# Layer 0's modulation on TensorE: weight blocks as the stationary operand instead of the conditions

## The chip, the cores and the metric

The kernel runs on one core of a Trainium2 chip, as one launch. The metric is device time in microseconds (us), the median of several runs of the whole program. Engines are TensorE (PE; its weight loads are listed apart as PEld), VectorE (DVE), ScalarE (ACT), GpSimd (POOL) and SyncE (SP), whose queue issues most of the loads from HBM. Everything is fp32; "fp32r" is the same 32 bits in a form that TensorE multiplies in one pass instead of two.

## The reference, cut to what matters

A block of two layers over 2048 latent tokens and 256 context tokens, 1024 wide. Layer 0 is an attention layer whose input is normalised and then modulated; the shift and scale come from two condition vectors, `c` for the latent and `c_ctx` for the context tokens:

```python
def modulate(x, g, shift, scale):
    return rms_norm(x, g) * (1 + scale) + shift

def ada_params(cond, w, b):                 # w: 1024 x 3072
    m = jax.nn.silu(cond) @ w + b
    return jnp.split(m, 3, axis=-1)         # shift, scale, gate

# layer 0
mods_x = ada_params(c, ada_w[0], ada_b[0])
mods_c = ada_params(c_ctx, ada_w[0], ada_b[0])
hx = modulate(x, norm_g, shift_x, scale_x)
hc = modulate(ctx, norm_g, shift_c, scale_c)
px = hx @ w_in                              # all projections of layer 0
...
```

Nothing of layer 0 can be projected before shift and scale are known. The gates (the last third of `m`) and layer 1's modulation are needed much later and are computed elsewhere.

## The kernel before, in words

`first_mods` (L210 to L232) computes shift and scale of layer 0 for both conditions. It is the first work of the program. `cs` [128, 8, 2] holds the two conditions as columns, eight blocks of 128 input rows, after a SiLU. The weight `ada0` (1024 x 2048, 8 MB) comes in eight blocks k of 128 rows (1 MB each), every block in two halves h of 1024 columns (L219, SP queue). The blocks go round four slots of the buffer `start`, so block 4 waits until TensorE has read block 0. For each half, two matmuls (L221) take `cs[:, k, :]`, 128 rows x 2 columns, as the stationary operand and stream 512 columns of weights past it; four PSUM tiles `ada` (tag "mm", 5 buffers) hold 2 rows x 512 sums each over all eight k. An fp32 matmul runs as two passes, each with its own weight load, so the profile counts 64 for 32 matmuls. Then the four row tiles are copied to `rows` (L224, by turns on VectorE and ScalarE), and 16 small matmuls against a 2x2 identity (L227) turn 2 x 128 pieces into columns: `cols` (tag "tr", 3 buffers) gets 128 partitions x 2 columns for each of 16 column groups. VectorE copies them out as `mods` (L230), and `ada_mods` (L172) adds the bias and forms `shift` and `gs`, per partition, for `load_group`.

`load_group` (L277) brings four token tiles: load `xt`, normalise to `xn` (L206, L208), transpose by TensorE into "tr" tiles (L288), apply `gs` and `shift` from PSUM to `h` (L296 on ScalarE, L293 on VectorE), split `h` into a high and a low half (`ghl`, L48 and L53). `load_w` (L302) brings projection weights `wraw` (2 buffers) and splits them into `whi` on GpSimd (L50) and `wlo` on VectorE (L53). The projections are three fp32r matmuls a step (L57 to L59). `weight_transform` (L234) puts the Fourier layer's weights through a small DFT: it loads `wuT` pieces into the same buffer `start` (L243), adds and subtracts them on VectorE (L246, L247), multiplies on TensorE (L255 to L257), copies on ScalarE (L258, L259).

In this part of the kernel the order of the instructions on each engine and on the DMA queues is set by the framework's planner, which simulates the program's timeline; waits between engines follow from the data. Engines take their instructions strictly in that order. Only the attention phase, from some 800 us on, has an order written out by hand (`P2ORDER`).

Of the kernel before, what the change touches and what calls it, by code (L numbers as in the profile page):

```python
# [10 lines left out]
F32 = mybir.dt.float32  # L11
# [7 lines left out]
P = 128  # L19
D = 1024  # L20
KT = D // P
# [67 lines left out]
def block_kernel(ctx: ExitStack, tc: tile.TileContext, a):  # L89
    nc = tc.nc  # L90
    V, S, T, Q = nc.vector, nc.scalar, nc.tensor, nc.gpsimd
# [33 lines left out]
    ident = const.tile([P, P], F32, name="ident")  # L125
# [46 lines left out]
    def ada_mods(l, m, i):  # L172

        V.tensor_tensor(out=shift[:, i, :], in0=m[:, 0:8], in1=adab[:, l, 0:8], op=ALU.add)
        V.tensor_tensor(out=gs[:, i, :], in0=m[:, 8:16], in1=adab[:, l, 8:16], op=ALU.add)
        V.scalar_tensor_tensor(out=gs[:, i, :], in0=gs[:, i, :], scalar=1.0, in1=ngc[:, l, :],
                               op0=ALU.add, op1=ALU.mult)
# [32 lines left out]
    def first_mods(pool, buf, pp):  # L210

        cs = pool.tile([P, KT, 2], F32, name="cs")
        ld(cs, a["ccT"])
        S.activation(cs, cs, AF.Silu)
        acc = [pp.tile([P, 512], F32, name="ada", tag="mm", bufs=5) for _ in range(4)]
        for k in range(KT):
            aw = buf[:, (k % 4) * 2048:(k % 4 + 1) * 2048]
            for h in range(2):
                ld(aw[:, h * 1024:(h + 1) * 1024], a["ada0"][k * P:(k + 1) * P, h * 1024:(h + 1) * 1024])  # L219
                for q in (2 * h, 2 * h + 1):  # L220
                    T.matmul(acc[q][0:2, :], cs[:, k, :], aw[:, q * 512:(q + 1) * 512], start=k == 0, stop=k == KT - 1)  # L221
        rows = pool.tile([2, 4, 512], F32, name="rows")
        for q in range(4):
            (S.copy if q % 2 else V.tensor_copy)(rows[:, q, :], acc[q][0:2, :])  # L224
        cols = pp.tile([P, 4, P], F32, name="cols", tag="tr", bufs=3).rearrange("p a b -> p (a b)")
        for j in range(16):
            T.matmul(cols[:, 2 * j:2 * j + 2], rows[:, j // 4, (j % 4) * P:(j % 4 + 1) * P], ident[0:2, 0:2],  # L227
                     start=True, stop=True)
        m = pool.tile([P, 2, 16], F32, name="mods")
        V.tensor_copy(m, cols[:, 0:32].rearrange("p (j c) -> p c j", c=2))  # L230
        for c in range(2):
            ada_mods(0, m[:, c, :], c)  # L232
# [30 lines left out]
    with ExitStack() as ph:  # L263
        pp = ph.enter_context(tc.tile_pool(name="p1ps", bufs=4, reuse_waits="tile", space=PSUM))
# [6 lines left out]
        start = grp.tile([P, 2 * KT * G], F32, name="start", tag="ghl")  # L271
        with tc.tile_pool(name="p0", bufs=1, reuse_waits="tile", side="right") as p0:
            first_mods(p0, start, pp)
# [152 lines left out]
        for half in range(2):  # L426
# [4 lines left out]
            for kind, col in chunks:  # L431
                whi, wlo = load_w(col)
                for src, g in groups:
# [4 lines left out]
                    if kind == "g":  # L438
                        if src == 1:
                            continue  # L440
                        for m in range(4):
                            ps = pp.tile([P, 512], F32, name="mm", tag="mm", bufs=5)
                            cs = slice(m * P, (m + 1) * P)
# [59 lines left out]
    with ExitStack() as ph:  # L503
        pp = ph.enter_context(tc.tile_pool(name="p2ps", bufs=1, reuse_waits="tile", space=PSUM))
# [333 lines left out]
    with ExitStack() as ph:  # L838
        pp = ph.enter_context(tc.tile_pool(name="p3ps", bufs=2, reuse_waits="tile", space=PSUM))
# [31 lines left out]
        for g in TOKEN_GROUPS:  # L871
            cs = slice(g * G, (g + 1) * G)
            us = []
            for b in range(KT):
# [13 lines left out]
                h = up.tile([P, G], F32R, name="uh", tag="uh")  # L888
# [188 lines left out]
        with ExitStack() as pd:  # L1077
            pp = pd.enter_context(tc.tile_pool(name="p5ps", bufs=2, reuse_waits="tile", space=PSUM))
# [78 lines left out]
        pp = ph.enter_context(tc.tile_pool(name="p6ps", bufs=2, reuse_waits="tile", space=PSUM))  # L1157
# [180 lines left out]
```

## Time and profile before

| | us |
|---|---|
| runs, median | 2697.39 |
| runs, lowest and highest | 2694.66, 2704.54 |
| profiled execution, time | 2701.17 |
| profiled execution, span from the first to the last instruction | 2699.4 |
| TensorE busy in it | 2593.4 (96%) |
| VectorE, ScalarE, GpSimd busy | 1795.5, 1388.4, 1067.0 |

The time of a run includes a little around the span. Times in the views are us from the span's start. A timeline row gives start, duration, engine, line, operation, written tile and read tiles, shape, and how many instructions are merged in it; in brackets stands the idle time before it and what ended that. Waits and DMA issues are not counted as busy. Ends of matmuls are modelled, so distances between starts are more exact than ends.

### The profile page before, as it was taken

The numbers are of one execution on the slowest core, as the hardware profiler recorded it, in microseconds if no ns is written. First come the engines' busy times: TensorE is split into PE (matmuls) and PEld (weight loads), VectorE is DVE, ScalarE is ACT, GpSimd is POOL, SyncE is SP. The second block draws the span as 40 slices with busy tenths as digits, with TensorE's granted clock in tenths as the row PEclk, the third lists the DMA queues.
The fourth block names the chain that finished last, engine by engine and source line by source line (L and its number), as shares of the span: only waits on it lengthen the run. The fifth ranks groups of instructions, "written<-read, shape, count | busy, mean of one in ns | idle before, by whom it ended". The sixth has DMA issues, their size and how long they took to land.

```text
span 2699.4 us, 44939 instructions
## 1 busy us (share of the span) xinstructions
PE 2593.4 (96%) x15361; PEld 2248.5 (83%) x15361; DVE 1795.5 (67%) x3894; ACT 1388.4 (51%) x3721; POOL 1067.0 (40%) x984
## 2 busy tenths in 40 slices
PE   7899999999998999999999999999999999899998
PEld 3788887787886999999999999999877878688787
DVE  4653734647416888888888888888865444563765
ACT  3621212412216888888888888888824442231212
POOL 1031421233315997666556556566511222332000
PEclk9999999999998999999999999999999999999999
DMA  7547555476534443311151011110287666757542
GB/s 289 192 131 205 149 156 196 118 187 182 146 114 148 160 162 106 112 32 33 35 165 31 29 32 59 54 30 29 86 283 263 207 217 218 254 172 210 195 152 94
DMA packets 294855, 380.20 MB, mean 141 GB/s; under 512 B 26642, under 2 KB 178914, under 8 KB 294626
## 3 DMA queue, kind: packets, MB, share of 16 engines
q1 hardware_dynamic: 163844, 275.02, 31.5%
q10 hardware_dynamic: 125600, 93.38, 11.1%
q0 software_dynamic: 5184, 8.93, 1.2%
q8 instruction: 123, 2.02, 0.3%
q14 instruction: 104, 0.85, 0.1%
HBM read 258.62 MB, written 118.57 MB: 140 GB/s over the span
## 4 chain that ended last, share of the span: by engine, by line
PE 62%; DMA 6%; DVE 4%; issue 1%; ACT 1%; POOL 1%; SPq 0%; DVEq 0%; ACTq 0%; POOLq 0%
PE s L571 17%; PE ptr L671 9%; PE mm L57 7%; PE mm L58 7%; PE mm L59 7%; PE pv L57 5%; PE pv L59 5%; PE pv L58 5%; DMA hraw<-h 1%; DMA wraw<-in_wg 1%; DMA w0h<-wo0h 1%; DVE m L579 1%; DMA wraw<-wur 1%; DMA kB<-kB 1%; DMA rcp<-s1r 1%
## 5 line engine op out<-in xcount | busy, mean ns | idle before, releaser
L579 DVE TENSOR_REDUCE m<-s 128x1 f32<-128x512 f32 (+1 forms) x960 | 579.0, 632 | 170.4 <-PE s L571 162.5
L591 ACT ACTIVATE e<-s,nm 128x512 f32<-128x512 f32 (+1 forms) x960 | 614.1, 653 | 53.1 <-DVE nm L583 50.6
L675 ACT CAST th<-ptr 128x512 fp32r<-128x512 f32 x576 | 340.3, 591 | 135.0 <-PE ptr L671 118.8
L679 DVE TENSOR_TENSOR tl<-ptr,th 128x512 fp32r<-128x512 f32 x576 | 379.1, 681 | 37.3 <-ACT th L675 37.3
L671 PE MATMUL ptr<-ident,e 128*128 128x128 f32 x2304 | 346.7, 273 | 8.8 <-DVE tl L679 6.9
L633 POOL TENSOR_TENSOR e<-e 128x768 f32<-128x768 f32 x189 | 342.6, 1841 | 0.0
L671 PEld LDWEIGHTS ptr<-ident,e 128*128 128x128 f32 x2304 | 270.1, 140 | 37.1 <-DVE tl L679 5.7
L571 PE MATMUL s<-kB,qh 128*128 128x512 f32 (+1 forms) x768 | 285.3, 381 | 10.4 <-DMA kB<-kB 7.3
L50 POOL TENSOR_SCALAR whi<-wraw 128x1024 fp32r<-128x1024 f32 (+1 forms) x104 | 125.4, 1209 | 424.8 <-PE mm L58 123.3
L59 PE MATMUL mm<-whi,ghl 128*128 128x512 f32 x688 | 272.2, 397 | 3.8 <-DVE ghl L53 3.8
L57 PE MATMUL mm<-whi,ghl 128*128 128x512 f32 x688 | 271.9, 398 | 3.8 <-DVE ghl L52 1.9
L58 PE MATMUL mm<-wlo,ghl 128*128 128x512 f32 x688 | 272.1, 397 | 0.7 <-DVE wlo L53 0.7
L630 POOL TENSOR_SCALAR e<-e,rs 128x768 f32<-128x768 f32 x192 | 170.7, 914 | 255.8 <-DVE rs L606 246.7
L53 DVE TENSOR_TENSOR wlo<-wraw,whi 128x1024 fp32r<-128x1024 f32 (+1 forms) x104 | 132.3, 1275 | 183.3 <-POOL whi L50 181.4
L571 PE MATMUL s<-kB,ql 128*128 128x512 f32 (+1 forms) x768 | 252.3, 341 | 0.0
L630 POOL TENSOR_SCALAR e<-e,c 128x768 f32<-128x768 f32 x189 | 168.6, 909 | 139.0 <-ACT e L591 77.0
L333 POOL TENSOR_TENSOR t<-qn,rope 128x256 f32<-128x256 f32 (+1 forms) x128 | 112.3, 898 | 270.3 <-issue 127.5
L591 ACT ACTIVATION_READ_ACCUMULATOR e<-s,nm 128x1 f32 x960 | 201.9, 210 | 0.0
L57 PE MATMUL pv<-th,vAh 128*128 128x256 f32 x576 | 169.0, 293 | 0.2 <-ACT oT L644 0.2
L57 PE MATMUL pv<-th,vBh 128*128 128x256 f32 x576 | 165.5, 287 | 0.0
L571 PEld LDWEIGHTS s<-kB,qh 128*128 128x128 f32 x768 | 147.5, 192 | 19.2 <-DMA kB<-kB 6.1
L58 PE MATMUL pv<-tl,vAh 128*128 128x256 f32 x576 | 160.2, 278 | 0.0
(367 smaller groups left out, 6311.1 us busy)
## 6 DMA issues: line engine op xcount, KB each, us to landing
wraw<-in_w_in SPq DMA_DIRECT2D x56, 512.0 KB, 4.3
hraw<-h SPq DMA_DIRECT2D x96, 256.0 KB, 4.5
aw<-in_adaT SPq DMA_DIRECT2D x64, 256.0 KB, 3.6
g<-sg ACTq DMA_DIRECT2D x64, 256.0 KB, 3.0
gl<-g SPq DMA_DIRECT2D x64, 256.0 KB, 5.3
wraw<-in_wg SPq DMA_DIRECT2D x64, 256.0 KB, 4.2
kB<-kB SPq DMA_DIRECT2D x24, 384.0 KB, 3.8
start<-in_ada SPq DMA_DIRECT2D x16, 512.0 KB, 10.2
```

The lines of the kernel that those rows point to most:

```text
L53: (lo_eng or nc.vector).tensor_tensor(out=lo, in0=src, in1=hi.bitcast(F32), op=ALU.subtract)
L57: nc.tensor.matmul(out, lh, rh, start=start, stop=False)
L58: nc.tensor.matmul(out, lh, rl, start=False, stop=False)
L59: nc.tensor.matmul(out, ll, rh, start=False, stop=stop)
L571: T.matmul(ps[:, c - o:c - o + cw], l, r[c // KP][:, k:k + cw], start=(j == 0), stop=(j == len(self.terms) - 1))
L579: V.tensor_reduce(out=self.m3[:, i:i + 1], in_=self.segs[i][:, 0:SEG[i][1]], axis=AX.X, op=ALU.max)
L591: S.activation(self.e[:, o:o + w], self.segs[i][:, 0:w], AF.Exp, bias=self.nm, accum_out=self.s3[:, i:i + 1])
L630: eng.tensor_scalar(out=self.e[:, sg], in0=self.e[:, sg], scalar1=by, scalar2=1.0, op0=ALU.mult, op1=ALU.mult)
L633: eng.tensor_tensor(out=onto[:, sg], in0=onto[:, sg], in1=self.e[:, sg], op=ALU.add)
L671: T.transpose(self.tr[:, k, i, :], self.p.es[i][:, kt * P:(kt + 1) * P], ident)
L675: S.copy(self.th, self.tr.rearrange("p k i q -> p k (i q)"))
L679: V.tensor_tensor(out=self.tl, in0=self.tr.rearrange("p k i q -> p k (i q)"), in1=self.th.bitcast(F32), op=ALU.subtract)
```

## The change

The weights become the stationary operand: for every block k and each of the 16 groups of 128 weight columns, one matmul holds a 128 x 128 block of `ada0` and streams the two conditions past it as two columns. The sums come out as columns at once, in 32 columns of one PSUM tile `cols`, which is now allocated at the beginning; it collects over all k in one accumulation group, opened by the first matmul and closed by the last. The row tiles, their copies and the 16 matmuls against the identity are gone. Loads of weights, `mods` and what follows stay as they are.

```diff
-        acc = [pp.tile([P, 512], F32, name="ada", tag="mm", bufs=5) for _ in range(4)]
+        cols = pp.tile([P, 4, P], F32, name="cols", tag="tr", bufs=3).rearrange("p a b -> p (a b)")
         for k in range(KT):
             aw = buf[:, (k % 4) * 2048:(k % 4 + 1) * 2048]
             for h in range(2):
                 ld(aw[:, h * 1024:(h + 1) * 1024], a["ada0"][k * P:(k + 1) * P, h * 1024:(h + 1) * 1024])
-                for q in (2 * h, 2 * h + 1):
-                    T.matmul(acc[q][0:2, :], cs[:, k, :], aw[:, q * 512:(q + 1) * 512], start=k == 0, stop=k == KT - 1)
-        rows = pool.tile([2, 4, 512], F32, name="rows")
-        for q in range(4):
-            (S.copy if q % 2 else V.tensor_copy)(rows[:, q, :], acc[q][0:2, :])
-        cols = pp.tile([P, 4, P], F32, name="cols", tag="tr", bufs=3).rearrange("p a b -> p (a b)")
-        for j in range(16):
-            T.matmul(cols[:, 2 * j:2 * j + 2], rows[:, j // 4, (j % 4) * P:(j % 4 + 1) * P], ident[0:2, 0:2],
-                     start=True, stop=True)
+                for j in range(8 * h, 8 * h + 8):
+
+                    T.matmul(cols[:, 2 * j:2 * j + 2], aw[:, j * P:(j + 1) * P], cs[:, k, :],
+                             start=k == 0 and j == 0, stop=k == KT - 1 and j == 15)
         m = pool.tile([P, 2, 16], F32, name="mods")
         V.tensor_copy(m, cols[:, 0:32].rearrange("p (j c) -> p c j", c=2))
```

## Rows read from the trace of the kernel before

**Rows 1.** The page: span, and busy time of each engine.

```profile
span 2699.4 us, 44939 instructions
PE 2593.4 (96%) x15361; PEld 2248.5 (83%) x15361; DVE 1795.5 (67%) x3894; ACT 1388.4 (51%) x3721; POOL 1067.0 (40%) x984
```

**Rows 2.** Timeline, all engines, 0 to 75 us: start, duration, engine, line, operation.

```profile
11.40 15.46 PE L221 MATMUL ada<-start,cs 128*2 128x512 f32 x32 [11.40 <-DMA start<-in_ada]
12.21 0.13 PEld L221 LDWEIGHTS ada<-start,cs 128*2 128x2 f32 x1 [0.73 <-issue]
13.06 0.13 PEld L221 LDWEIGHTS ada<-start,cs 128*2 128x2 f32 x1 [0.73 <-issue]
...
15.11 0.09 PEld L221 LDWEIGHTS ada<-start,cs 128*2 128x2 f32 x1 [0.34 <-issue]
15.54 0.09 PEld L221 LDWEIGHTS ada<-start,cs 128*2 128x2 f32 x1 [0.34 <-issue]
...
28.04 1.88 PE L221 MATMUL ada<-start,cs 128*2 128x512 f32 x4 [1.18 <-DMA start<-in_ada]
30.67 12.18 PE L221 MATMUL ada<-start,cs 128*2 128x512 f32 x28 [0.75 <-DMA start<-in_ada]
```

**Rows 3.** Windows: us, busy by engine (count), granted clock, DMA share, GB/s.

```profile
34.00:37.00 3.00, 3.00 (x8) 0.59 (x7) 0.00 (x0) 0.00 (x0) 0.00 (x0) 1.00 1.03 412
48.30:48.60 0.30, 0.25 (x3) 0.01 (x1) 0.30 (x4) 0.00 (x0) 0.00 (x0) 1.00 1.06 376
48.60:48.90 0.30, 0.00 (x0) 0.00 (x0) 0.30 (x5) 0.00 (x0) 0.00 (x0) 0.70 1.11 382
85.00:90.00 5.00, 3.60 (x31) 3.20 (x29) 2.32 (x7) 5.00 (x26) 0.00 (x0) 1.00 0.30 95
102.00:103.00 1.00, 0.00 (x0) 0.00 (x0) 0.00 (x0) 0.00 (x0) 0.00 (x0) 1.00 0.96 367
107.00:108.00 1.00, 1.00 (x5) 1.00 (x5) 0.97 (x2) 0.00 (x0) 0.00 (x0) 0.50 1.08 374
```

**Rows 4.** Timeline of weight loads and matmuls, 42 to 49; line L227's durations (min/median/max).

```profile
44.77 2.75 PEld L227 LDWEIGHTS cols<-ident,rows 2*128 2x128 f32 x24 [0.17 <-issue]
47.90 0.65 PE L288 MATMUL tr<-ident,xn 128*128 128x128 f32 x4 [0.28 <-DVE mods L230]
L227 PEld LDWEIGHTS cols<-ident,rows x32: 181/187/188, 42.8 to 47.3; 2*128 2x128 f32 x32
```

**Rows 5.** Timeline, 47 to 56: from the columns to the first projection matmul.

```profile
47.65 0.19 DVE L230 COPY mods<-cols 128x32 f32<-128x32 f32 x1 [0.61 <-PE cols L227]
47.82 0.69 DVE L246 TENSOR_TENSOR start<-start 128x512 f32<-128x512 f32 x1
...
48.80 1.22 DVE L53 TENSOR_TENSOR wlo<-wraw,whi 128x1024 fp32r<-128x1024 f32 x1
...
50.61 0.24 DVE L176 SCALAR_TENSOR_TENSOR gs<-gs,ngc 128x8 f32<-128x8 f32 x2
50.80 0.81 ACT L296 ACTIVATE h<-tr,shift,gs 128x128 f32<-128x128 f32 x2 [4.35 <-DVE gs L176]
...
55.27 0.77 PE L57 MATMUL mm<-whi,ghl 128*128 128x512 f32 x1
```

**Rows 6.** Timeline of TensorE's matmuls: the longest idle time up to 110 us.

```profile
106.98 0.80 PE L255 MATMUL wur<-start 128*128 128x129 f32 x2 [6.05 <-DVE start L247]
```

**Rows 7.** Timeline of weight loads at clock 0.50 (to 113.4) and 1.00.

```profile
107.36 0.55 PEld L256 LDWEIGHTS wur<-start 128*128 128x128 f32 x2
107.79 0.55 PEld L257 LDWEIGHTS wur<-start 128*128 128x128 f32 x2
113.69 0.30 PEld L256 LDWEIGHTS wur<-start 128*128 128x128 f32 x2
113.91 0.30 PEld L257 LDWEIGHTS wur<-start 128*128 128x128 f32 x2
```

**Rows 8.** The view of line L221: durations in ns (min/median/max).

```profile
L221 PE MATMUL ada<-start,cs x64: 590/592/1057, 11.4 to 42.3; 128*2 128x512 f32 x64
```

## Prediction

> **What bounds the kernel now.** I began with the page's first lines: TensorE is busy for 2593.4 of 2699.4 us [rows 1]. So what is gained or lost at the start should be found again at the end unless a later idle stretch of TensorE swallows it. The change touches only the first 50 us, so I read the timeline of that stretch next. The 64 passes of L221 (32 matmuls, two passes each in fp32) start at 11.40, when the first weight block lands, and end at about 42.8: the last 28 passes, from 30.67, take 12.18 us, so they start every 0.43 us [rows 2]. On the way TensorE waits for weights twice, up to 28.04 and up to 30.67 [rows 2]; the DMA engines are full meanwhile [rows 3]. Then L227 turns the rows into columns, 32 passes in two stretches with 8 transposes between them, until 47.6, and VectorE copies the result at 47.65 [rows 4, 5]. From there a chain runs to the first projection matmul at 55.27: shift and gs, h, the cast, L57 [rows 5]. After it TensorE is hardly idle until it waits for the second half of the Fourier weights at 106.98 [rows 6]. What sets the time of the change is therefore when the sums over `ada0` are complete, plus that chain.
>
> **Removed.** The 64 passes of L221 with 512 moving columns; four copies of rows, two on VectorE and two on ScalarE, done by the time L227 goes on; and 32 passes of L227. From the first pass to the end of L227 that is 47.6 - 11.4 = 36.2 us, waits for DMA and 8 transposes included.
>
> **Added.** 8 blocks k x 16 column groups = 128 matmuls, 256 passes. Each loads a stationary block of 128x128 and streams two columns. The nearest row in shape is L227 itself, with 128 stationary columns and two moving ones: 24 loads in 2.75 us, the last alone 0.187, so (2.75 - 0.187)/23 = 0.111 us from one pass to the next [rows 4]. It has only 2 partitions where the change has 128. But L256, 128x128 stationary with 64 moving columns, starts its pairs 0.22 us apart from the next line's at full clock, 0.11 us a pass [rows 7]: full partitions cost no more. A pass is thus paid by its weight load, and the two moving columns cost next to nothing. At full clock the stream costs 256 x 0.111 = 28.4 us, less than the 36.2 us now.
>
> **The clock decides.** All turns on whether this stream gets 2.4 GHz or 1.2 GHz. At the lower level the same weight loads cost twice as much: L256 starts at 107.36 and L257 at 107.79, two passes in 0.43 us, 0.215 each, at a granted clock of 0.50 [rows 3, 7]. Then 256 x 0.215 = 55.0 us. The trace has two observations. First, the kernel begins at the lower level: the passes of L221 start 0.85 us apart at 12.21 and 13.06, but 0.43 apart from 15.11 on [rows 2]. (The granted-clock column shows 1.00 for that beginning, so I trust the durations there, where the longest pass is 1057 ns and the median 592 [rows 8].) Dense passes of 512 columns raised it. Second, L227 with its two-column passes ran almost without a gap to 47.6, and four transposes to 48.55; the granted clock fell from 1.00 to 0.50 inside 48.60:48.90, when TensorE had been empty for no more than a few tenths [rows 3, 4]. Two other places show that short idleness alone doesn't do that: in 85:90 it was idle for 1.4 us of 5 and kept 1.00, and in 102:103, without a single matmul, it still had 1.00 [rows 3]. So the row says that back-to-back weight loads with two moving columns do not hold the clock; all the less should they raise it from the low level where the kernel starts. What speaks against: L227 uses 2 partitions, the change 128. No row shows two columns on 128 partitions for that long. I take the low level for the whole stream.
>
> The Trainium skill's page "TensorE: Matmul & The Clock Gate", section "Why this matters for your kernels", advises to keep TensorE continuously busy, without idle gaps between bursts, and the clock stays up. By that rule the new stream, which has no gaps, would run at 2.4 GHz; the fall at 48.7 directly behind a nearly gapless stretch does not agree with it, and the first rival below is worked out for the case that it holds. The same page's section "LDWEIGHTS (loading the stationary operand)" gives a weight load as its columns over 1.2 GHz, 107 ns for 128 of them, at either clock. The 0.111 us agrees with it, the 0.215 us does not; by it the stream would be an estimated 27 us.
>
> **The sum.**
> 1. First pass at 11.40, as now: the load of the first block is untouched. With 55.0 us the last pass ends at 66.4. Waits for weights vanish: a block k has 32 passes, 6.9 us, while a block of 1 MB takes about 2.6 us at the 400 GB/s of these windows [rows 3], and the slot of k=0 is free for k=4 some 20 us before that is wanted. Columns complete at 66.4 instead of 47.6: +18.8 us.
> 2. Transposes of the first token tile: in L227's time now, 8 of them. A transpose is one pass with the same 128-column load, so 8 in the stream at the low level take 8 x 0.215 = 1.7; if they come after, some of it lies on the chain. Bounds 0 and 1.7, I take +0.9. `cols` now holds one of the three "tr" buffers from the start on; the first tile needs the other two, so this costs nothing until the third transposes, which already wait for the copy of mods today.
> 3. The chain from the columns to the first L57 takes 7.6 us (47.65 to 55.27). VectorE does other work inside it: a wlo split of 1.22 and four or five sums of the Fourier weights at 0.69, one of them in the rows, 4.0 to 4.7 us, and an xn [rows 5]. Those inputs have landed long before 66.4, so in the new kernel this work can be done while TensorE is still in its stream. VectorE works in the order that the planner fixes, which I can't see: bounds 0 and -4.6, which leaves some 3 us for gs, h and the cast. I take -2.7.
> 4. Loads that queue behind a waiting load on the SP queue: the last `ada0` load now waits for the slot of k=3, until 11.4 + 4 x 6.9 = 39, and the Fourier weights, which lie in the same buffer, until k=4 to 6 are done, at most 59.7. Behind them are xt, two wraw loads and rope. All land before 66.4, and POOL's whi and VectorE's wlo are done by then too: 0, with +3 as the bound if the third and fourth wraw stand behind all of the Fourier loads.
> 5. Later absorption: between 55 and 107 the largest idle piece of TensorE is 6.05 us before L255 [rows 6]. It ends with loads into `start` that wait for the first half of the Fourier transform, so it moves along with everything else: 0, with -2 as a bound.
>
> Together +18.8 + 0.9 - 2.7 = +17.0 us. The profiled execution took 2701.17 us, 1.8 more than its span, so it would become 2718.2; it lies 3.8 above the median of the runs, 2697.39. On the median I forecast **2714.4 us**, 0.6% slower. With the bounds of steps 2 to 5 the forecast's own range is +11 to +24, 2708 to 2721.
>
> **Rivals.**
> *Full clock (not slower).* The stream has no gaps, the clock rises as it does now around 14.5 and stays. By 26.9 k=0 to 3 are done as now (14 passes at 0.215, the rest at 0.111 give 27.1), the waits for k=4 end at 28.04 and 30.67 as now, and the seven half blocks left are 7 x 16 passes x 0.111 = 12.4, so 43.1 against 47.6: -4.5, part of which the wlo split and DMA full until 47.6 take back. About 2694 us, within 0.5%. For it: TensorE is given work all the time, on all 128 partitions. Against it: the fall at 48.7. It decides from the point where the loads alone, without streamed columns, hold the clock.
> *Clock in between.* The level rises late, or alternates as transposes and loads mix; half the stream at each level is 41.7 us, columns at about 53 to 55, +6 to +8 before the shorter chain, so +3 to +8: 2700 to 2705, within 0.5%.
> *Planner reorders.* The stream is costed differently by whoever orders the queues, and wraw, xt or transposes end up behind loads that wait for slots: +3 of step 4, no shorter chain, and another idle stretch like the 6 us of [rows 6]: +25 to +30, 2722 to 2727.
> *Nothing done:* that the matmuls aren't 128 pairs of passes is excluded by the diff; L227 shows two passes a matmul (32 for 16).
>
> **How the numbers follow.** Half clock throughout 0.66, full clock 0.18, in between 0.09, reordered and worse 0.07. 0.5% is 13.5 us, about what a measurement of this kernel can tell from no change; the border is 2710.9. Of the forecast's own range some three quarters lies above it: slower 0.66 x 0.75 + 0.07 = 0.56. Same: 0.66 x 0.25 + 0.18 + 0.09 less a little = 0.41; faster 0.03, since even the full clock gives only -4.5. The range: 2692 takes in the full-clock case but for its lower end, 2722 the forecast's upper end; outside are most of the last case and some of the first rival, about 0.13.
>
> **What would show it.** In the profile after: passes of the new line at 0.21 to 0.22 us with loads of about 330 ns (right), or 0.11 and 190 ns (full clock); granted clock 0.5 until about 4 us into the projections; the copy of mods at about 66 to 68; the first L57 4 to 6 us after it; the wait before L255 near 124 and still about 6 us long. I am wrong if the loads take 190 ns, or if they take 330 and the lost time is still not there behind L255.

## The result, and the profile after

| | us |
|---|---|
| before, median (4 runs) | 2697.61 |
| after, median (4 runs, 2711.66 to 2715.77) | 2714.19 |
| ratio, 95% interval | 1.0058, 1.004 to 1.0076 |
| after, profiled execution: time and span | 2714.98, 2713.2 |

The changed kernel is 0.6% slower, 16.6 us on the medians. The page of after has the span and the busy time that answer to [rows 1]:

```profile
span 2713.2 us, 45256 instructions
PE 2614.6 (96%) x15521; PEld 2294.3 (85%) x15521; DVE 1790.8 (66%) x3892; ACT 1387.0 (51%) x3719; POOL 1062.1 (39%) x984
```

TensorE is busy for 21 us more, though the 32 passes of L227 are gone. The view of the new line (durations in ns, min/median/max, then first and last start) says where:

```profile
L222 PEld LDWEIGHTS cols<-cs,start x256: 286/333/333, 11.5 to 65.9; 128*128 128x128 f32 x128
L222 PE MATMUL cols<-cs,start x256: 342/352/352, 11.5 to 65.9; 128*128 128x2 f32 x128
  DMA start<-in_ada: 11.5, 1
```

256 passes from 11.5 to 65.9 are 0.213 us each. The loads take 333 ns, as those of L256 and L257 in the kernel before did from 107 to 113 us, at a granted clock of 0.50. The only wait for weights is the one before the first pass; the two of [rows 2] are gone. Yet the window view puts the granted clock of the same stretch at 1.00 (its columns as in [rows 3]):

```profile
20.00:40.00 20.00, 20.00 (x95) 20.00 (x95) 7.00 (x16) 3.88 (x7) 2.80 (x3) 1.00 1.03 401
```

Column and durations can't both be right, and the first experiment decides between them. The timeline behind the stream answers to [rows 5] and [rows 6]:

```profile
65.94 2.61 PEld L283 LDWEIGHTS tr<-ident,xn 128*128 128x128 f32 x12
66.33 0.19 DVE L225 COPY mods<-cols 128x32 f32<-128x32 f32 x1 [4.89 <-PE cols L222]
66.87 0.28 DVE L176 SCALAR_TENSOR_TENSOR gs<-gs,ngc 128x8 f32<-128x8 f32 x2
67.28 0.46 ACT L291 ACTIVATE h<-tr,shift,gs 128x128 f32<-128x128 f32 x1 [40.20 <-PE tr L283]
70.47 0.42 PEld L283 LDWEIGHTS tr<-ident,xn 128*128 128x128 f32 x4 [1.93 <-DVE h L288]
71.22 0.47 PE L57 MATMUL mm<-whi,ghl 128*128 128x512 f32 x1
...
123.05 0.80 PE L250 MATMUL wur<-start 128*128 128x129 f32 x2 [4.77 <-DVE start L242]
```

`mods` is copied at 66.33 instead of 47.65 (+18.7). The chain to the first L57 takes 4.9 us instead of 7.6, since wlo and the sums of the Fourier weights no longer stand in it: L57 starts at 71.22 instead of 55.27 (+15.95). The wait for the second half of the Fourier weights ends at 123.05 instead of 106.98 (+16.1): up to here the delay passed through unchanged.

### The profile page after: what moved, and what is told of

It reads as the page before. It is cut to its first block, busy times and chain, and to the rows that moved or that the text cites. A ratio compares the mean times of both kernels' runs of the same rounds, so it can differ in the third digit from the quotient of the medians.

```text
span 2713.2 us, 45256 instructions
## 1 busy us (share of the span) xinstructions
PE 2614.6 (96%) x15521; PEld 2294.3 (85%) x15521; DVE 1790.8 (66%) x3892; ACT 1387.0 (51%) x3719; POOL 1062.1 (39%) x984
## 4 chain that ended last, share of the span: by engine, by line
PE 60%; DMA 7%; DVE 3%; ACT 1%; issue 1%; POOL 1%; SPq 0%; ACTq 0%; DVEq 0%; POOLq 0%
PE s L566 17%; PE ptr L666 9%; PE mm L57 6%; PE mm L58 6%; PE mm L59 6%; PE pv L57 5%; PE pv L59 5%; PE pv L58 5%; DMA hraw<-h 2%; DMA wraw<-in_wg 1%; DVE m L574 1%; DVE wlo L53 1%; DMA kB<-kB 1%; DMA gl<-g 0%; DMA w0h<-wo0h 0%
## 5 line engine op out<-in xcount | busy, mean ns | idle before, releaser
L566 PE MATMUL s<-kB,qh 128*128 128x512 f32 (+1 forms) x768 | 285.8, 381 | 10.5 <-DMA kB<-kB 7.4
L57 PE MATMUL mm<-whi,ghl 128*128 128x512 f32 x688 | 270.7, 396 | 3.6 <-DVE ghl L52 2.0
L57 PE MATMUL pv<-th,vAh 128*128 128x256 f32 x576 | 169.4, 294 | 0.2 <-ACT oT L639 0.2
L57 PE MATMUL pv<-th,vBh 128*128 128x256 f32 x576 | 165.3, 287 | 0.0
```

Of the source, the lines that this page charges most:

```text
L57: nc.tensor.matmul(out, lh, rh, start=start, stop=False)
L566: T.matmul(ps[:, c - o:c - o + cw], l, r[c // KP][:, k:k + cw], start=(j == 0), stop=(j == len(self.terms) - 1))
```

## The experiments

Each kernel is the changed one with the edit shown; e8 starts from the kernel before, e9 and e10 are the two kernels themselves, e11 is e6 once more. The letters A to E in the expectations name the theories that a run can tell apart; A is that of the prediction, that the clock follows what is streamed behind the loads. Ratios are to runs of the kernel before on the same chip.

### The clock raised beforehand (e1)

```diff
+        wt = pool.tile([P, 512], F32, name="warm")
+        V.memset(wt, 1.0)
+        wps = pp.tile([P, 512], F32, name="wps", tag="mm", bufs=5)
+        for i in range(9):
+            T.matmul(wps, ones, wt, start=i == 0, stop=i == 9 - 1)
         cs = pool.tile([P, KT, 2], F32, name="cs")
```

> The changed kernel with nine fp32 matmuls of 512 columns (on constants, their sums unused) put ahead of the stream, while TensorE waits for the first weights, so that the stream starts at the high clock. Theory A (streamed columns hold the clock; two are too few): the first loads of the stream take 190 ns, then they fall back to 333 ns within a few us; 1 to 6 us less than the changed kernel, 2708 to 2714. Rival B (0.215 us is simply the price of a 128x128 fp32 load with two columns, the granted clock of 1.00 shown in the stream is true): 333 ns from the first pass on, 2712 to 2716. Rival C (a stream without gaps holds a clock that is up, it only cannot raise it): 190 ns throughout, columns at about 43 us, 2688 to 2696.

Measured: 2706.06 us, ratio 1.0034 (1.0021 to 1.0046), 2 us under the range of theory A. The view of the stream's line, for 11 to 16 and for 16 to 22 us, and the windows between:

```profile
L227 PEld LDWEIGHTS cols<-cs,start x39: 186/192/333, 11.4 to 15.9; 128*128 128x128 f32 x39
...
L227 PEld LDWEIGHTS cols<-cs,start x30: 333/333/333, 15.7 to 21.9; 128*128 128x128 f32 x30
...
14.00:15.00 1.00, 1.00 (x11) 1.00 (x10) 0.00 (x0) 0.00 (x0) 0.00 (x0) 1.00 1.03 414
15.00:15.50 0.50, 0.50 (x6) 0.50 (x6) 0.00 (x0) 0.29 (x1) 0.00 (x0) 0.93 1.01 401
15.50:16.00 0.50, 0.50 (x5) 0.50 (x4) 0.00 (x0) 0.50 (x1) 0.00 (x0) 0.50 1.13 451
```

The stream began at the high clock with loads of 192 ns and lost it at about 15.5, while TensorE and its loads were busy without a gap. From there every load of the stream took 333 ns, and the column shows 0.50. So 333 ns is the low clock, not the price of this form (B falls), and being gapless did not hold it here (C falls). It follows too that the 1.00 in the changed kernel's stream is no measurement: there the column shows 1.00 until the first change of the clock is recorded.

The Trainium skill's page "TensorE: Matmul & The Clock Gate", section "Why this matters for your kernels", asks for TensorE to be kept busy without idle gaps; this stream was, and the clock fell all the same, so for two streamed columns the runs contradict that rule as I read it. The Trainium skill's section "LDWEIGHTS (loading the stationary operand)" on the same page gives a load one duration and names no level of the clock for it; the 192 and 333 ns of one and the same load here show two.

### Each matmul twice (e4)

```diff
                 for j in range(8 * h, 8 * h + 8):
-                    T.matmul(cols[:, 2 * j:2 * j + 2], aw[:, j * P:(j + 1) * P], cs[:, k, :],
-                             start=k == 0 and j == 0, stop=k == KT - 1 and j == 15)
+                    for r in range(2):
+                        T.matmul(cols[:, 2 * j:2 * j + 2], aw[:, j * P:(j + 1) * P], cs[:, k, :],
+                                 start=k == 0 and j == 0 and r == 0, stop=k == KT - 1 and j == 15 and r == 1)
```

> The changed kernel with each matmul of the stream issued twice (so the sums come out doubled): 256 passes more. If the stream stands alone on the path that sets the end, at 0.215 us a pass (theory A, and B): 55 us more than the changed kernel, 2767 to 2770, and the copy of mods near 121 us. Rival D (most of the loss is a different order of the queues behind it, and the stream's length has slack): clearly less, under 2755.

Measured: 2769.88 us, ratio 1.0274 (1.0248 to 1.03), 55.7 us above the changed kernel.

```profile
L222 PEld LDWEIGHTS cols<-cs,start x512: 288/333/338, 11.3 to 120.3; 128*128 128x128 f32 x171
...
120.78 0.19 DVE L225 COPY mods<-cols 128x32 f32<-128x32 f32 x1 [15.56 <-PE cols L222]
```

The columns came 54.5 us later and the end 55.7: the stream lies on the path that sets the end with its full length. D falls.

### Wider streams: 64, 16 and 128 columns (e2, e3, e6)

The conditions are repeated so that each load is followed by more columns; below with 64, the others differ in the repeats and in how many PSUM tiles hold the sums.

```diff
+        csw = pool.tile([P, KT, 32, 2], F32, name="csw")
+        V.tensor_copy(csw, cs.unsqueeze(2).to_broadcast([P, KT, 32, 2]))
...
-                    T.matmul(cols[:, 2 * j:2 * j + 2], aw[:, j * P:(j + 1) * P], cs[:, k, :],
+                    T.matmul(cols[h][:, 64 * j:64 * j + 64], aw[:, (8 * h + j) * P:(8 * h + j + 1) * P],
+                             csw[:, k].rearrange("p r c -> p (r c)"),
```

> The changed kernel with each pair of conditions repeated 32 times, so that every weight block is followed by 64 columns instead of 2; the sums are the same, only the first two of 64 are used. Loads are as many and as large. Theory A: the columns raise the clock after some us as in the kernel before, loads fall from 333 to 190 ns and a pass to about 0.111 us, because 64 columns fit beside the next load; columns complete at 43 to 48 us, 2690 to 2699. Rival B: the pass is still 0.215 us or more, 2714 or slower. Rival C: 333 ns and 0.215 us as well, since there are no more gaps or fewer than in the stream of two columns, 2714.

> As the kernel with 64 columns, with 16. Theory A gives either end or something between: like two columns (2714) if 16 do not raise the clock, like 64 (2690 to 2699) if they do, and the loads tell which: 333 or 190 ns. Rivals B and C: 0.215 us a pass, 2714.

> The same 128 columns for each weight block without raising the clock first. Theory A: a raise some us after the first pass, as for the mixed passes of 129, 64 and 128 columns in the kernel before, which began at the low level and reached the high one 6.5 us later; columns at about 45 us, 2692 to 2700. Rival E: 333 ns and 0.215 us throughout, 2710 to 2716, as with 2, 16 and 64 columns.

Measured: 64 columns 2713.55 us, ratio 1.0067 (1.0047 to 1.0087); 16 columns 2710.97 us, 1.0054 (1.0036 to 1.0072); 128 columns 2689.81 us, 0.9966 (0.9956 to 0.9976). The loads of the three whole streams, in the order 64, 16 and 128 columns, then for 128 columns two stretches, 11 to 16 and 22 to 28 us:

```profile
L223 PEld LDWEIGHTS cols<-csw,start x256: 287/333/333, 11.4 to 65.8; 128*128 128x128 f32 x128
...
L223 PEld LDWEIGHTS cols<-csw,start x256: 288/333/338, 11.4 to 65.7; 128*128 128x128 f32 x128
...
L223 PEld LDWEIGHTS cols<-csw,start x256: 190/192/338, 11.4 to 45.2; 128*128 128x128 f32 x128
L223 PEld LDWEIGHTS cols<-csw,start x22: 288/333/338, 11.4 to 15.9; 128*128 128x128 f32 x22
L223 PEld LDWEIGHTS cols<-csw,start x56: 192/192/192, 21.8 to 28.0; 128*128 128x128 f32 x56
```

My expectation for 64 columns was wrong: they changed nothing, nor did 16. With 128 columns behind the same loads the clock rose after some 5 us of the stream, the loads fell to 192 ns and the sums were complete at about 45.5, 20 us sooner. Same loads, same number, same bytes: what was streamed behind them made the difference. (The number of PSUM tiles differs too, two for 64 columns and four for 128. Two tiles alone do not keep the clock low: e7 below has two, and half of its stream ran at the high level.) With e1 that shows the cause. The 2689.81 us are 2 us under the range expected for e6.

### Clock raised, then 64 or 128 columns (e7, e5)

The nine matmuls of e1 ahead of the stream of e2 and of e6.

> Clock raised first, then 64 columns for each block. 64 columns did not raise the clock from the low level; here is asked if they hold it. Theory A: either 190 ns throughout (2690 to 2698) or a fall as with two columns (2703 to 2714); Rival E: the fall.

> Clock raised ahead of the stream by nine matmuls on constants, and 128 streamed columns for each weight block (the two conditions repeated 64 times; only the first two sums are used). Theory A (the streamed columns decide the clock): it stays up, loads of 190 ns, 0.111 to 0.115 us a pass, columns at about 42 to 45 us, 2690 to 2698. Rival E (a stream of 128x128 fp32 loads loses or never gets the high clock whatever is streamed behind each load): loads go from 190 to 333 ns within some us as with two columns, 2706 to 2714.

Measured: 64 columns 2698.93 us, ratio 0.9996 (0.9987 to 1.0005); 128 columns 2688.48 us, 0.9959 (0.9946 to 0.9972), 1.5 us under the expected range. For 64 columns, TensorE's timeline, two windows, and the loads in 16 to 22 and in 40 to 66 us:

```profile
12.27 14.40 PE L228 MATMUL cols<-csw,start 128*128 128x64 f32 x128
29.01 1.94 PE L291 MATMUL tr<-ident,xn 128*128 128x128 f32 x8 [2.34 <-DVE rr L195]
32.92 27.41 PE L228 MATMUL cols<-csw,start 128*128 128x64 f32 x128
...
27.00:28.00 1.00, 0.00 (x0) 0.00 (x0) 0.78 (x5) 0.99 (x2) 0.00 (x0) 0.91 1.02 401
28.00:28.50 0.50, 0.00 (x0) 0.00 (x0) 0.48 (x2) 0.20 (x1) 0.21 (x1) 0.50 1.03 410
...
L228 PEld LDWEIGHTS cols<-csw,start x56: 192/192/192, 15.8 to 22.0; 128*128 128x128 f32 x56
...
L228 PEld LDWEIGHTS cols<-csw,start x95: 333/333/333, 39.8 to 59.8; 128*128 128x128 f32 x95
```

A surprise: the first 128 passes held the high clock to their end, 14.4 us of them; then transposes that waited for VectorE stood between the halves of the stream, the clock fell in the 2.34 us of idleness, at about 27.8, and the second 128 passes, of the same kind, took 27.4 us. In this trace streaming 64 columns held the clock where it was high and did not raise it where it was low. With 128 columns (e5) it fell between the halves too, at about 30 us, and was raised again at about 37. In e6 and e11, where TensorE was idle for only 1.37 and 1.50 us between the halves, it did not fall (granted clock 1.00 from 26 to 45 us in e6). No run here varied the idle time alone, so its share in these falls stays open.

### The kernel before with the raised clock, and both kernels once more (e8 to e11)

> The kernel before with the same nine matmuls ahead of its stream, so that its own first passes run at the high clock. All theories: the passes of the first 3 us take 0.43 instead of 0.85 us, but TensorE then waits longer for weights, since the DMA engines are full: at most 1.7 us off, 2694 to 2699. It says how much of a gain of the other three belongs to the raised clock alone.

> The kernel before, unchanged, profiled once more. Between the first matmul of layer 0's output projection (1975 us in the first trace) and the first write of the output (2566) the kernels of this study differ by up to 10 us, though they differ only in the first 50 us. If that is variation from execution to execution, this trace differs from the first one by several us in the same stretch and its first 1975 us agree within 1 us. If it is the order of the queues, which is the same in both, the stretch takes the same time within 1 us.

> The changed kernel, unchanged, profiled once more, for the same question. In both cases the first 1975 us come out as in its first trace: stream 11.5 to 66, output projection 15 us later than in the kernel before. Variation: the end differs by several us. Order: the end differs by under 1 us.

> The kernel with 128 streamed columns and no raised clock beforehand, unchanged, with more rounds, since it is the one that beats both. Its start should again be 5 us ahead of the kernel before behind the Fourier weights and 10 us at the output projection; 2687 to 2692, a ratio of 0.995 to 0.998.

Measured: e8 2693.65 us, ratio 0.9983 (0.9973 to 0.9994), just under its range; e9 2702.68 and e10 2714.54 us (one execution each); e11 2690.99 us, ratio 0.9969 (0.996 to 0.9979). How far each profiled execution is behind the first one of before at four places (differences of starts in the traces, us): the last L255 (122.4 in before), the first matmul of layer 0's output projection (1975.4), the first write of the output (2566.1), and the span:

| | last L255 | output projection | first write | span |
|---|---|---|---|---|
| before again (e9) | +3.3 | +6.1 | +1.5 | +1.5 |
| after | +16.8 | +15.3 | +13.8 | +13.8 |
| after again (e10) | +17.1 | +12.8 | +13.4 | +13.4 |
| clock raised, two columns (e1) | +17.5 | +14.1 | +4.3 | +4.3 |
| each matmul twice (e4) | +72.8 | +71.8 | +70.9 | +70.9 |
| 128 columns (e6) | -5.3 | -10.5 | -11.5 | -11.6 |
| 128 columns again (e11) | -5.4 | -6.5 | -8.9 | -8.9 |
| clock raised, 64 columns (e7) | +8.4 | +5.8 | -3.1 | -3.1 |
| before, clock raised (e8) | +0.9 | 0.0 | -8.2 | -8.2 |

The delay of the start is there at the Fourier weights and still there 1850 us later. How large it is there is less certain than one trace suggests: between the two traces of one and the same kernel lie 6.1 us (before) and 2.5 us (after) at the output projection, though I had expected 1 us at most for before.

The stretch between the output projection and the first write differs by 4.6 us between the two traces of before (+6.1 to +1.5), by 2.1 us between those of after, whose ends are only 0.4 us apart. By what I had expected, e9 speaks for variation from execution to execution and e10 for the order, so the two do not decide. The runs with the nine matmuls ahead do stand out: the stretch takes 580.9 to 582.5 us in e1, e7 and e8 and 585.9 in e5, and 585.5 to 591.3 in the nine other traces. The window view of it for before and for e8 (columns as in [rows 3]):

```profile
1975.40:2566.10 590.70, 562.92 (x2746) 467.96 (x2746) 316.40 (x565) 177.59 (x393) 140.31 (x148) 0.97 0.69 225
1975.40:2557.90 582.50, 557.22 (x2746) 463.11 (x2746) 315.10 (x565) 178.19 (x393) 139.47 (x148) 0.98 0.70 228
```

TensorE has the same 2746 matmuls in both, and in these two traces takes them in the same order, as VectorE does its instructions; it is busy for 5.7 us less in e8, at a granted clock of 0.98 instead of 0.97. So the order of these engines is not what makes e8 8.2 us quicker there, and at least part of it goes with how long the clock was low so late in the program. Over the 55 executions of before that belong to the experiments, the time goes with the clock as well: the four with a mean granted clock of 0.981 took 2702.9 us on average, the four with 0.986 2696.9. Why kernels with the nine matmuls at the start should be granted more some 2000 us later, no run shows.

For e8 this means that its gain of 0.17% is not shown to come from its start, which was slower in its trace: TensorE waited 3.83 us for weights up to 29.57, the copy of `mods` came at 51.1 instead of 47.65 and L57 at 57.75 instead of 55.27. The same holds for most of e1's gain: its stream ended 3.7 us sooner, 1 us or so of that is left at the output projection, less than the two traces of the changed kernel differ there, and the rest of its 8 us lies in that late stretch.

The second trace of before held something on the clock that I had not asked for. There L227's second stretch took 4.20 us instead of the 2.75 of [rows 4]; the timeline of its loads and two windows:

```profile
44.90 4.20 PEld L227 LDWEIGHTS cols<-ident,rows 2*128 2x128 f32 x24 [0.17 <-issue]
...
45.50:46.00 0.50, 0.50 (x6) 0.50 (x6) 0.00 (x0) 0.50 (x2) 0.33 (x1) 1.00 1.06 406
46.00:46.50 0.50, 0.50 (x5) 0.50 (x4) 0.15 (x1) 0.28 (x3) 0.00 (x0) 0.51 1.07 410
```

The clock fell in the middle of the two-column passes here, at about 46.0, with TensorE fully busy; in the first trace it fell just behind them.

## Why the prediction was right, point by point

- **The clock decides.** Right, with the cause as predicted: e1 shows the fall inside a gapless two-column stream, e6 the rise with the same loads. The reading of the fall at 48.7 carried it. My doubt about 2 against 128 partitions is settled by e1: 128 partitions do not hold it either.
- **Step 1, the stream.** 55.0 us and an end at 66.4 were forecast; the last pass starts at 65.9 and `mods` is copied at 66.33 (+18.7 for a forecast of +18.8). 0.215 us a pass was 0.213.
- **Step 2, transposes.** +0.9 was forecast, next to nothing came. All twelve stand behind the stream and run beside the chain; ScalarE's first h, at 67.28, is released by a transpose when gs had been ready since 67.15, so some 0.1 us of them is visible, and it is part of the 4.89 us of step 3.
- **Step 3, the chain.** -2.7 forecast, 4.89 against 7.62 us measured, -2.7. That the amount fits is partly luck: VectorE's other work left the chain entirely, which the prediction priced at -4.6, but what remained took 4.9 us and not some 3. ScalarE now has a pass for xn (1.04 us from 68.49) between two of its h, and the four transposes in front of L57 wait until 70.47 for VectorE's h.
- **Step 4, the SP queue.** 0 forecast, 0 measured: no wait for wraw, xt or Fourier weights is left in front of L57.
- **Step 5, later absorption.** 0 forecast; the wait at L255 moved by 16.1 and shrank from 6.05 to 4.77 us, while two shorter ones for ScalarE grew, from 1.8 to 4.0 us in all. e4's 55.7 us for 54.5 say the same of the whole path.
- **The sum.** +17.0 forecast, +15.95 at the first L57, +13.8 in the profiled span, +16.6 on the medians. The missing 1 us at L57 is step 2. That the median came out within 0.2 us of 2714.4 is luck: the stretch behind 1975 us alone varies by more. The lower end of the forecast's own range was added up wrongly: 18.8 - 4.6 - 2 is +12.2, not +11; no result hangs on it.
- **A sign that was wrong.** I named a granted clock of 0.5 in the stream and in the first 4 us of the projections. The column shows 1.00 in the stream, since it had nothing recorded yet, and the projections began at the high level: the four transposes at 70.47 take 0.42 us and L57's first load 190 ns. The twelve transposes ahead of them, 128 columns each, had run at the low level (2.61 us). In e4 the projections began at the low level all the same, and in e10, the changed kernel's second trace, they began at the high one and fell back at about 72.4, so this was not a property of the change.
- **Rivals.** Full clock: e6 shows the stream at the high level all but some 5 us, and 2690 us for a forecast of 2694. In between is what e7 shows: half of the stream at each level, +5.8 us at the output projection for a forecast of +3 to +8; its 2699 us hold the late gain of the runs with nine matmuls as well. Reordering at a cost of its own did not come.

Streaming 128 columns beats both kernels: 2689.81 and 2690.99 us in ten runs each, 0.9966 and 0.9969 of the kernel before, and 2688.48 us with the clock raised beforehand. It computes each sum 64 times and is still quicker than the changed kernel, because at the high clock the 128 columns stream beside the next load. Against the kernel before, two rows of e6 show what its start gains, to be compared with [rows 5]:

```profile
46.68 0.15 DVE L228 COPY mods<-cols 128x8 f32<-128x8 f32 x1
51.25 0.77 PE L57 MATMUL mm<-whi,ghl 128*128 128x512 f32 x1
```

The sums are complete at about 45.5 instead of 47.6, and the chain behind them is shorter by about as much again, so L57 starts 4.0 us sooner. The end is 8 to 12 us earlier in the two traces, and 10.2 and 8.4 us on the medians; where the part beyond the start's 4 to 5 us comes from is not shown.

## What to carry to other kernels

Swapping the operands turns a stream paid by its columns into one paid by its weight loads; before that, look in the profile what the clock did behind a stretch of just such passes. Read the clock from the duration of a load that occurs at both levels, not from the column alone, above all at the start of a program. If a stream of loads must run at the high clock, streaming more columns than are needed can be free, as 128 were here. Before a gain of a few us is put down to an edit, find the point of the program where it arises: e1 and e8, with nine matmuls at the start, gained most of their time some 2000 us later.

## What the runs showed of the hardware that was not expected

A 128x128 fp32 load with a stream behind it took 0.111 to 0.113 us from pass to pass at the high clock, whether 64 or 128 columns followed, and 0.213 us at the low clock with 2, 16, 64 or 128. Streams of 64 columns behaved differently by their history: at the high clock they kept it for 14.4 us (e7), at the low clock they stayed low for 54 us (e2), one trace each. And the granted-clock column showed 1.00 at the beginning of every kernel here whose first loads took 333 ns (11.5 to 65.9 us in the changed kernel).
